# Columns of the modulation at another pace, summed two blocks past their request, and two later steps in the gates and the inverse

## The chip, the cores and the metric

The kernel runs on one core of a Trainium2 chip. The metric is the device time of one execution in microseconds (us). Before the change it is 1945.58 us, the median of three runs (1941.93 to 1946.73). A core has five engines with a queue of instructions each: TensorE (PE) for matmuls, VectorE (DVE), ScalarE (ACT), GpSimd (POOL) and SyncE (SP); here SP issues the transfers (DMA). Each engine works through its own queue in order, and waits at an instruction until what that instruction needs is there.

## The reference

One decoder layer for 256 positions of width 2048, in float32. Every part is normed and modulated by nine vectors of length 2048, which come from the conditioning `c` by one large matrix:

```python
x = x + 1/2 * gate1 * SwiGLU_1(mod(norm(x)))
x = x + gate2 * W_out [ FoX(heads 0..7) || GatedDeltaNet(heads 0..7) ]
x = x + 1/2 * gate3 * SwiGLU_2(mod(norm(x)))

# the gated delta rule, per head and chunk of 64
decay = jnp.exp(jnp.where(incl, g[..., :, None] - g[..., None, :], -jnp.inf))
lower = jnp.where(strict, jnp.einsum("bhnid,bhnjd->bhnij", kb, k) * decay, 0.0)
t_inv = lax.linalg.triangular_solve(eye + lower, jnp.broadcast_to(eye, lower.shape), ...)
u = t_inv @ vb
w = t_inv @ (kb * jnp.exp(g)[..., None])
```

A last norm follows. The decays `g` and the factors `beta` come from 24 extra columns of the mixer's input projection, through softplus and sigmoid: these are "the gates" below. The feed-forward parts are called FFN1 and FFN2, and what stands between them the mixer.

## The kernel before

**The weights** are cut into tiles of 128 x 128, and eight of them, in the order in which PE uses them, make a block of 512 KB. There are 674 blocks. For each, SP issues one transfer (`wraw`, line 125), ACT rounds it to the fast matmul format (`whi`, line 128), DVE forms the rest (`wlo = wraw - whi`, line 140), and PE multiplies with both halves. At most four buffers stand behind each of the three steps, with a few more for `wraw` in part of the kernel. So each block passes through four queues, and PE is late as soon as one `wlo` is.

Blocks 0 to 112 are the first gate/up part of FFN1 (28 pairs of feature tiles), 112 to 168 the down part for these, 168 to 232 the second gate/up part (16 pairs, four blocks each), 232 to 264 its down part. Blocks 264 to 378 are the mixer's input projection, 378 to 410 its output projection, 410 to 674 FFN2. In the profiled execution `wlo` of block 66 is made at 207 us, of 90 at 268, 112 at 330, 168 at 482, 232 at 659, 264 at 741, 378 at 1135 and 410 at 1229.

**The columns.** The matrix of the modulation is read as 142 columns of 1 MB (`adat`, line 262); each is multiplied by the conditioning and summed by one DVE instruction (line 266). `ada_col` requests a column; `Stream.next` calls it at a rate per block that the table `RATE` gives from block to block: 0.45 means 45 columns in 100 blocks. Where `W.late` is false, the sum is issued with the request; where it is true (from the mixer on), the sum is put into a list, and `settle` issues it behind `wlo` of the second block after (`BEHIND = 2`). The changed lines are in `Stream.next`, in the table, and in three lines of the mixer.

**The epilogue of a feature pair** in the second gate/up part: PE has left `pg` and `pu` (line 485 with `whi`, 486 with `wlo`), ACT copies one half to `mg` and DVE adds the other into `tg` and `tu` (497); ACT applies silu, DVE multiplies `tu` by `tg` (520), ACT rounds the product to `hid` and DVE forms its rest (504).

**The mixer.** While PE works through the projections, chains of small steps are dealt out between its tiles: Python generators for the gates and the keys ("k"), for each head of the delta rule ("gdn") and of the forgetting attention ("fox"), and for the output. Each `yield` names a gap in us by an internal clock that counts PE's tiles (`tick`, 0.35 us for each); a chain's next step is written down when that clock has passed its gap. A scheduling layer then orders the instructions of each engine by its own rules; `issue_after(i)` keeps an instruction behind instruction i in that order, `W.last` being the latest weight request and `W.split` the latest `wlo`.

- `gates` rounds the 24 extra columns (`x`, line 836), transposes them (`pcol`, 845), applies softplus and sigmoid, and sums with triangular matmuls (`prow`, 878).
- `decays`, `row_of` and `fetch_rows` (`rowd` to `rw`, 904, and to `x`, 929) make the decay matrices, with exponentials on ACT (918, 941).
- `keys` and `solve` make the lower triangle `Ln` for four heads at a time; `solve` sends its 16 x 16 blocks through memory (`ld`), inverts them by 15 products and reductions on DVE (1015, 1016), sends the result out (`lt<-x`, 1021) and back in another layout (`x<-lt`, 1025), and masks it into `U0` (1029). For the first half it then fetches the rows of the second (`x<-rowd`, 929).
- `gdn` of each head uses `U0`: `pu` (1051, 1053; another tile than the `pu` of FFN1), transposes `pvq` (1056) of the convolved queries and values `qv` (962, with silu on ACT), and goes on to `pn` (1093) and `put` (1105).
- `fox` of each head transposes its probabilities `ppt` (1209), which ACT made by an exponential (1204).

Of the kernel before, what the change touches and what calls it, by code (L numbers as in the profile page):

```python
# [13 lines left out]
ALU = mybir.AluOpType  # L14
# [18 lines left out]
GR = 24  # L33
NEG = -1e30

RATE = ((0, 0.5), (28, 0.25), (33, 0.5), (49, 0.25), (56, 0.5), (66, 0.2), (90, 0.0), (112, 0.5), (168, 0.45), (232, 0.26), (264, 0.0), (288, 0.295), (384, 0.0), (424, 0.16))
N_BIG, N_GDN = 3, 3
N_FIRST = 2
AHEAD = 4
# [4 lines left out]
LATER = 8  # L44
SLOTS = (3, 11)
BEHIND = 2

HA = 128 + 16
HS = 4 * HA
# [29 lines left out]
def woven(ap):  # L79

    return ap.rearrange("p (a b) -> p b a", a=2)
# [12 lines left out]
class Stream:  # L94


    def __init__(self, nc, w, raw, hi, lo):
        self.nc, self.w, self.raw, self.hi, self.lo = nc, w, raw, hi, lo
        self.order = []
        self.more = None  # L100
        self.h = self.l = self.last = None
        self.owed, self.side, self.quiet = 0.0, lambda: None, False
        self.tc, self.hold, self.held = None, None, []
        self.first = []
        self.lead = None
        self.late, self.owing = False, []

    def settle(self, upto=N_TILES):

# [21 lines left out]
    def next(self, mat, k, n, width=1):  # L131
        i = len(self.order)
        if i % WB == 0:
            nc = self.nc
            b = i // WB
            r, lo = self.first.pop(0) if self.first else self.block(b)
            self.l = lo.tile([P, WB * P], F32R, name="wlo")
            pace = [r_ for r_ in RATE if r_[0] <= b][-1][1]
            with self.behind():
                lo_ = nc.vector.tensor_tensor(self.l, r, self.h.bitcast(F32), ALU.subtract)  # L140
            with self.tc.issue_after(lo_.ins):
                self.settle(b - BEHIND)
            self.split = lo_.ins
            self.owed += 0.0 if self.quiet else pace
            while self.owed >= 1.0:
                self.owed -= 1.0
                self.side()
        for d in range(width):
            self.order.append((mat, k, n, width, d))
        o = (i % WB) * P  # L150
        h, l = self.h[:, o : o + width * P], self.l[:, o : o + width * P]
        return (h, l) if width == 1 else (woven(h), woven(l))
# [3 lines left out]
def layer_kernel(ctx: ExitStack, tc: tile.TileContext, xrow, c, adaw, cols, cst, w, out, order, dbg=None):  # L156
    nc = tc.nc
    V, A, G, PE = nc.vector, nc.scalar, nc.gpsimd, nc.tensor
# [18 lines left out]
    def psf(name="psf"):  # L177
        return sm2.tile([P, 512], F32, name=name, tag="psf")
# [6 lines left out]
    W = Stream(nc, w, raw, hi, lo)  # L185
# [40 lines left out]
    def C(name, lo_=0, n=None):  # L226
        o, wd = CST[name]
        return cstt[:, o + lo_ : o + (wd if n is None else lo_ + n)]

    def L(name, lo_=0, n=None):  # L230
        o, wd = COL[name]
        return colt[:, o + lo_ : o + (wd if n is None else lo_ + n)]
# [218 lines left out]
    def pt(name):  # L451
        return tmp.tile([P, T], F32, name=name, tag="pt", bufs=4)
# [301 lines left out]
    def mixer():  # L754
# [76 lines left out]
        def gates(ps):  # L831

            yr = x[:, 8]
            d = pt("ey")
            s = norm1.scaled(d, ps)
            A.activation(yr[R], d[R], AF.Identity, bias=s[R])
            y, ny, e, em, t0, q = (x[:, j, : 2 * GR].rearrange("p (t r) -> p t r", t=2) for j in range(10, KD))
            coef = tiny.tile([P, GR + PAD["hid"]], F32, name="coef", bufs=1)[:, :GR]
            tc.keep_in_program_order(A.activation(coef, L("alog"), AF.Exp))
            V.tensor_scalar(coef, coef, -1.0, None, ALU.mult)  # L840
            yield 4.0
            pc = psf("pcol")
            pcv = pc[:, : 2 * GR].rearrange("p (t r) -> p t r", t=2)
            for t in range(2):
                PE.transpose(pcv[:, t], yr[R, t * P : (t + 1) * P], ident[R, :GR])
            both = lambda c_: c_.unsqueeze(1).to_broadcast([P, 2, GR])
            V.tensor_tensor(y, pcv, both(L("gbias")), ALU.add)
            V.tensor_tensor(y, y, both(C("sgn")), ALU.mult)
            V.scalar_tensor_tensor(ny, y, -1.0, y, ALU.mult, ALU.min)
            A.activation(e, ny, AF.Exp)  # L850
            V.tensor_scalar(em, y, 0.0, None, ALU.min)
            A.activation(em, em, AF.Exp)

            S = ny
            V.tensor_scalar(t0, e, 2.0, None, ALU.add)
            V.reciprocal(t0, t0)
            V.tensor_tensor(S, e, t0, ALU.mult)
            V.tensor_tensor(t0, S, S, ALU.mult)
            V.tensor_scalar(q, t0, 1.0 / 17.0, None, ALU.mult)
            for n in (15, 13, 11, 9, 7, 5, 3):  # L860
                V.scalar_tensor_tensor(q, q, 1.0 / n, t0, ALU.add, ALU.mult)
            V.scalar_tensor_tensor(q, q, 1.0, S, ALU.add, ALU.mult)
            V.tensor_scalar(y, y, 0.0, None, ALU.max)
            V.scalar_tensor_tensor(y, q, 2.0, y, ALU.mult, ALU.add)
            V.tensor_tensor(y, y, both(coef), ALU.mult)

            V.tensor_scalar(t0, e, 1.0, None, ALU.add)
            V.reciprocal(t0, t0)
            V.tensor_tensor(colS[:, :, 4], em[:, :, 16:24], t0[:, :, 16:24], ALU.mult)
            yield 8.0  # L870

            fox_, gdn_ = slice(0, NH), slice(NH, 2 * NH)
            pr = psf("prow")
            po = psf("pcum")
            pcs = po[:, : 6 * NH].rearrange("p (t q r) -> p t q r", t=2, q=3)
            for t in range(2):
                sl = slice(t * P, (t + 1) * P)
                PE.matmul(pr[:NH, T + t * P : T + (t + 1) * P], y[:, t, gdn_], C("tri64"), start=True, stop=True)
                PE.matmul(pr[:NH, sl], y[:, t, fox_], C("tri"), start=True, stop=(t == 0))
                if t:  # L880
                    PE.matmul(pr[:NH, sl], y[:, 0, fox_], L("ones"), start=False, stop=True)
            for t in range(2):
                PE.matmul(pcs[:, t, 1], C("tri64"), y[:, t, gdn_], start=True, stop=True)
                PE.matmul(pcs[:, t, 2], C("tru64"), y[:, t, gdn_], start=True, stop=True)
                PE.matmul(pcs[:, t, 0], C("tri"), y[:, t, fox_], start=True, stop=(t == 0))
                if t:
                    PE.matmul(pcs[:, t, 0], L("ones"), y[:, 0, fox_], start=False, stop=True)
            rt = x[:, 8:10].rearrange("p a t -> p (a t)")[:NH]
            A.copy(rt, pr[:NH])
            nc.sync.dma_start(rows, rt)  # L890
            V.tensor_copy(colS[:, :, 0:2], pcs[:, :, 0:2])
            A.activation(colS[:, :, 2:4], pcs[:, :, 1:3], AF.Exp)
            V.tensor_tensor(nbeg, colS[:, :, 4], colS[:, :, 2], ALU.mult)
            V.tensor_scalar(nbt, colS[:, :, 4], -1.0, None, ALU.mult)
            V.tensor_scalar(ng, colS[:, :, 1], -1.0, None, ALU.mult)
            yield 2.0
            fetch_rows(0)
            yield 1.0
# [25 lines left out]
        def fetch_rows(half):  # L924

            rowk[half] = x[:, 4 * half : 4 * half + 4]
            src = rows[4 * half : 4 * half + 4, T:]
            with tc.issue_after(W.last):
                nc.sync.dma_start(rowk[half], src.unsqueeze(0).to_broadcast([P, 4, T]))
# [59 lines left out]
        def solve(half):  # L989


            hs4, n = slice(4 * half, 4 * half + 4), 2 * NH // 2
# [14 lines left out]
            blk, xt_, pr = (x[B, j] for j in range(4, 7))  # L1007
            with tc.issue_after(W.last):
                nc.sync.dma_start(blk, ld[ht].rearrange("n b e -> (n b) e"))
            yield 6.0  # L1010
            G.memset(xt_, 0.0)
            G.memset(xt_[:, 0:256:17], 1.0)
            bv, xv, pv = (t_.rearrange("p (i j) -> p i j", i=16) for t_ in (blk, xt_, pr))
            for i in range(1, 16):
                V.tensor_tensor(pv[:, :i, :i], xv[:, :i, :i], bv[:, i, :i].unsqueeze(1).to_broadcast([8 * n, i, i]), ALU.mult)
                V.tensor_reduce(xv[:, :i, i], pv[:, :i, :i], mybir.AxisListType.X, ALU.add)
                if i % 3 == 0:
                    yield 1.2
# [266 lines left out]
                if h + 1 < NH:  # L1285
                    rowf[h + 1] = row_of(h + 1, 0, "f")

        W.late = True
        first = project([("gt", 0)] + [("qkv", NH + h) for h in range(3)], norm1)
        start("k", -1, gates(first[0]))  # L1290
        for h in range(3):
            have_keys(h, first[1 + h], norm1)
# [37 lines left out]
    if dbg is None or "mix" in dbg:  # L1330
        mixer()
# [154 lines left out]
```

## Time and profile before

| what | value |
| --- | --- |
| median of three runs | 1945.58 us |
| the profiled execution | 1944.62 us, its span 1942.8 us |
| PE, share of the span | 98% |
| DVE | 81% |
| ACT | 54% |
| POOL | 3% |
| read from memory | 512.89 MB, 266 GB/s over the span |

The span is what the engines' records cover; the execution has 1.8 us around it. "Busy" counts records of work, not the time in which an engine waits at the head of its queue. A view of waits sums an engine's idle time by the instruction that stood and by what it stood for. A timeline has a row for each instruction with its start and its length, and in brackets the idle time ahead of it and what ended that.

### The profile page before, as it was taken

What the parts mean: (1) busy time and instruction counts of PE and PEld (TensorE: products, weight loads), DVE (VectorE), ACT (ScalarE), POOL (GpSimd) and SP (SyncE); (2) the same over time, 40 slices, a digit from 0 to 9 for tenths busy, and PEclk for the clock granted to TensorE, in tenths of its full rate; (3) what the DMA queues carried; (4) which work ended last, traced back from release to release, by engine and by line L of the source; (5) the groups of instructions that cost most, each with busy time, mean ns of one, the idle gap of its engine ahead of it and who ended that gap; (6) DMA issues with size and microseconds to landing.
All of it is one profiled execution on the core that took longest, in us unless ns stands there. A gap on an engine that the chain in (4) does not pass through costs nothing. (4 is left out here: it accounts for less than half of the span.)

```text
span 1942.8 us, 33800 instructions
## 1 busy us (share of the span) xinstructions
PE 1902.1 (98%) x13086; PEld 1774.6 (91%) x13087; DVE 1570.4 (81%) x2455; ACT 1047.1 (54%) x1668; POOL 53.5 (3%) x55
## 2 busy tenths in 40 slices
PE   9999999999999999999999999999999999999998
PEld 7999999988889899888989999999999999999997
DVE  6999978989999999878987989887777665666654
ACT  7444545433444557847656756665554445555553
POOL 0000000000000021000000002000000000000011
PEclk9999999999999999999999999999999999999999
DMA  9988867999999886585677557677777665666663
GB/s 376 354 348 329 325 227 257 399 377 375 365 360 366 327 287 225 199 333 198 207 275 274 204 196 247 203 256 275 263 262 251 227 204 198 203 199 202 200 201 120
DMA packets 129490, 519.58 MB, mean 267 GB/s; under 512 B 18217, under 2 KB 21545, under 8 KB 111153
## 3 DMA queue, kind: packets, MB, share of 16 engines
q1 hardware_dynamic: 129330, 517.42, 74.3%
q8 instruction: 103, 1.69, 0.3%
q14 instruction: 57, 0.47, 0.1%
HBM read 512.89 MB, written 4.47 MB: 266 GB/s over the span
## 5 line engine op out<-in xcount | busy, mean ns | idle before, releaser
L140 DVE TENSOR_TENSOR wlo<-wraw,whi 128x1024 fp32r<-128x1024 f32 x674 | 819.1, 1221 | 264.3 <-ACT whi L128 263.3
L128 ACT CAST whi<-wraw 128x1024 fp32r<-128x1024 f32 x674 | 698.9, 1044 | 523.3 <-PE pd L489 152.9
L489 PE MATMUL pd<-hid,whi 128*128 128x512 f32 x1408 | 461.7, 382 | 0.0
L490 PE MATMUL pd<-hid,wlo 128*128 128x256 f32 x1408 | 384.2, 273 | 2.1 <-DVE wlo L140 2.1
L266 DVE CUSTOM_DVE_ANT_0 adat<-adat,cs,colt 128x2048 f32<-128x2048 f32 x142 | 332.9, 2344 | 7.3 <-DMA adat<-in_ada_dram 7.3
L485 PE MATMUL pg<-hs,whi 128*128 128x512 f32 x912 | 302.7, 382 | 0.5 <-DVE shc L433 0.5
L485 PE MATMUL pu<-hs,whi 128*128 128x512 f32 x912 | 302.4, 382 | 0.0
L489 PEld LDWEIGHTS pd<-hid,whi 128*128 128x128 f32 x1408 | 266.3, 189 | 36.8
L490 PEld LDWEIGHTS pd<-hid,wlo 128*128 128x128 f32 x1408 | 270.3, 192 | 4.0 <-DVE wlo L140 3.9
L486 PE MATMUL pu<-hs,wlo 128*128 128x256 f32 x912 | 249.7, 274 | 5.8 <-DVE wlo L140 5.5
L486 PE MATMUL pg<-hs,wlo 128*128 128x256 f32 x912 | 249.8, 274 | 0.0
L571 PE MATMUL pgu<-hs,wlo 128*128 128x256 f32 x896 | 240.3, 278 | 7.5 <-DVE wlo L140 7.2
L569 PE MATMUL pgu<-hs,whi 128*128 128x256 f32 x896 | 245.0, 277 | 0.4 <-ACT whi L128 0.3
L570 PE MATMUL pgu<-hs,whi 128*128 128x256 f32 x896 | 244.5, 276 | 0.0
L485 PEld LDWEIGHTS pg<-hs,whi 128*128 128x128 f32 x912 | 172.6, 189 | 24.3 <-ACT shc L432 0.7
L485 PEld LDWEIGHTS pu<-hs,whi 128*128 128x128 f32 x912 | 172.6, 189 | 23.4
L486 PEld LDWEIGHTS pu<-hs,wlo 128*128 128x128 f32 x912 | 175.0, 192 | 8.6 <-DVE wlo L140 8.4
L571 PEld LDWEIGHTS pgu<-hs,wlo 128*128 128x128 f32 x896 | 168.6, 193 | 10.5 <-DVE wlo L140 10.4
L486 PEld LDWEIGHTS pg<-hs,wlo 128*128 128x128 f32 x912 | 175.1, 192 | 1.5
L569 PEld LDWEIGHTS pgu<-hs,whi 128*128 128x128 f32 x896 | 172.7, 193 | 1.1 <-ACT whi L128 0.5
L570 PEld LDWEIGHTS pgu<-hs,whi 128*128 128x128 f32 x896 | 172.8, 193 | 0.2 <-DVE hs L383 0.2
L798 PE MATMUL pp<-hs,whi 128*128 128x256 f32 x592 | 170.8, 289 | 0.2 <-ACT whi L128 0.2
(344 smaller groups left out, 2644.9 us busy)
## 6 DMA issues: line engine op xcount, KB each, us to landing
wraw<-in_w_dram SPq DMA_DIRECT2D x674, 512.0 KB, 4.4
adat<-in_ada_dram SPq DMA_DIRECT2D x142, 1024.0 KB, 7.9
xr<-in_xr_dram SPq DMA_DIRECT2D x4, 512.0 KB, 4.9
adaf<-in_ada_dram SPq DMA_DIRECT2D x4, 512.0 KB, 8.2
xd<-x SPq DMA_DIRECT2D x4, 512.0 KB, 7.2
rw<-rowd SPq DMA_DIRECT2D x16, 128.0 KB, 5.5
x<-xd SPq DMA_DIRECT2D x4, 512.0 KB, 5.3
out_dram<-o SPq DMA_DIRECT2D x8, 256.0 KB, 2.8
```

The costliest lines, as they stand in the source:

```text
L128: self.cast = self.nc.scalar.copy(self.h, r).ins
L140: lo_ = nc.vector.tensor_tensor(self.l, r, self.h.bitcast(F32), ALU.subtract)
L266: V.tensor_tensor_reduce(t, t, cs, 1.0, L("adab", q, 1), ALU.mult, ALU.add, mod[:, q : q + 1])
L485: PE.matmul(ps, wt[0], both, start=(k == 0), stop=False)
L486: PE.matmul(ps[:, T:], wt[1], part(k, HI), start=False, stop=(k == KD - 1))
L489: PE.matmul(ps, wt[0], act.rearrange("p q (a b) -> p q b a", a=2), start=first, stop=False)
L490: PE.matmul(ps[:, :T], wt[1], woven(act[:, 0]), start=False, stop=last)
L569: PE.matmul(o, wh, part(k, HI), start=first and s == 0, stop=False, skip_group_check=skip)
L570: PE.matmul(o, wh, part(k, LO), start=False, stop=False, skip_group_check=skip)
L571: PE.matmul(o, wl, part(k, HI), start=False, stop=last, skip_group_check=skip)
L798: PE.matmul(pp[i][:, :T], wh, hh, start=(k == 0), stop=False)
```

## The change

The table of rates has other values in three stretches: 0.2 columns per block go on from block 66 to 112 (before, to 90, and none from there to 112), 0.39 instead of 0.45 from 168 to 232, 0.25 instead of 0.26 from 232 to 264. In blocks 66 to 112 the sums come two blocks past the request, as they did from the mixer on. In the gates the internal clock's gap ahead of the transposes is 7 us for 4, in the inverse the gap ahead of its first product is 8 us for 6, and that product is kept behind the latest `wlo`.

```diff
-RATE = (... (56, 0.5), (66, 0.2), (90, 0.0), (112, 0.5), (168, 0.45), (232, 0.26), (264, 0.0), ...)
+RATE = (... (56, 0.5), (66, 0.2), (112, 0.5), (168, 0.39), (232, 0.25), (264, 0.0), ...)
+LATE = (66, 112)
-        self.late, self.owing = False, []
+        self.late, self.pinned, self.owing = False, False, []
@@ Stream.next
             b = i // WB
+            self.late = self.pinned or LATE[0] <= b < LATE[1]
@@ gates
-            yield 4.0
+            yield 7.0
             pc = psf("pcol")
@@ solve
-            yield 6.0
+            yield 8.0
             G.memset(xt_, 0.0)
             for i in range(1, 16):
-                V.tensor_tensor(pv[:, :i, :i], xv[:, :i, :i], bv[:, i, :i].unsqueeze(1).to_broadcast([8 * n, i, i]), ALU.mult)
+                with tc.issue_after(W.split) if i == 1 else nullcontext():
+                    V.tensor_tensor(pv[:, :i, :i], xv[:, :i, :i], bv[:, i, :i].unsqueeze(1).to_broadcast([8 * n, i, i]), ALU.mult)
@@ the mixer
-        W.late = True
+        W.late = W.pinned = True
```

Counted in DVE's order, the columns by stretches of blocks are, before and after: 29 and 29 up to block 66, 5 and 6 to 90, 1 and 4 to 112, 27 and 27 to 168, 29 and 25 to 232, 7 and 7 to 264, 28 and 29 to 410, 12 and 11 to 500, 4 and 4 to the end. ACT's order has 35 table loads before and 37 after. The changed kernel's line numbers are two higher, three from the inverse on.

DVE in the second gate/up part, before, from the 181st `wlo` on (the names carry buffer numbers; `adat` is a column's sum, which also reads out into `mod`):

```order
L140 TENSOR_TENSOR wlo_5959<-wraw_5955,whi_5957 128x1024
L497 TENSOR_TENSOR tu_5941<-pu_5845,mg_5945 128x256
L140 TENSOR_TENSOR wlo_5981<-wraw_5977,whi_5979 128x1024
L520 TENSOR_TENSOR tu_5941<-tu_5941,tg_5940 128x256
L504 TENSOR_TENSOR hid_5950<-tu_5941,hid_5950 128x256
L266 ISA adat_5983,mod_124<-adat_5983,cs_86,colt_87 128x2048
L266 ISA mod_124 128x1
L140 TENSOR_TENSOR wlo_6006<-wraw_6002,whi_6004 128x1024
```

The same place after the change, again from the 181st `wlo`:

```order
L142 TENSOR_TENSOR wlo_5968<-wraw_5964,whi_5966 128x1024
L268 ISA adat_5970,mod_124<-adat_5970,cs_86,colt_87 128x2048
L268 ISA mod_124 128x1
L499 TENSOR_TENSOR tu_5950<-pu_5857,mg_5954 128x256
L142 TENSOR_TENSOR wlo_5993<-wraw_5989,whi_5991 128x1024
L522 TENSOR_TENSOR tu_5950<-tu_5950,tg_5949 128x256
L142 TENSOR_TENSOR wlo_6015<-wraw_6011,whi_6013 128x1024
L506 TENSOR_TENSOR hid_5959<-tu_5950,hid_5959 128x256
L268 ISA adat_6017,mod_124<-adat_6017,cs_86,colt_87 128x2048
```

Before, one `wlo` stands between the evacuation of `tu` and the column; after, a column stands ahead of the evacuation, and the next one behind two `wlo`.

SP in the first half of the inverse, before, behind the 302nd weight request (`rw` and `rowd` are rows of the decays):

```order
L125 DMA wraw_9656<-in_w_dram 128x1024
L1021 DMA lt_8294<-x_85 64x256
L904 DMA rw_9689<-rowd_8288 128x256
L125 DMA wraw_9692<-in_w_dram 128x1024
L1025 DMA x_85<-lt_8294 128x8x16
L262 DMA adat_9698<-in_ada_dram 128x2048
L125 DMA wraw_9731<-in_w_dram 128x1024
L125 DMA wraw_9772<-in_w_dram 128x1024
L929 DMA x_85<-rowd_8288 128x4x256
L125 DMA wraw_9803<-in_w_dram 128x1024
```

The same steps after the change, behind the 307th request:

```order
L126 DMA wraw_9890<-in_w_dram 128x1024
L1024 DMA lt_8294<-x_85 64x256
L126 DMA wraw_9920<-in_w_dram 128x1024
L126 DMA wraw_9952<-in_w_dram 128x1024
L1028 DMA x_85<-lt_8294 128x8x16
L264 DMA adat_9958<-in_ada_dram 128x2048
L931 DMA x_85<-rowd_8288 128x4x256
L126 DMA wraw_10039<-in_w_dram 128x1024
```

The three steps stand five to six weight requests later. Two requests instead of one stand between `lt<-x` and `x<-lt`, and none instead of two between `x<-lt` and `x<-rowd`.

PE at the gates' transposes, before (`pp` is a projection, `pcol` the transposes):

```order
L798 MATMUL pp_8816<-hs_125,whi_8849 128x256
L799 MATMUL pp_8816<-hs_125,whi_8849 128x256
L845 MATMUL pcol_8776<-colt_87,x_85 128x24 x2
L800 MATMUL pp_8816<-hs_125,wlo_8851 128x256
L798 MATMUL pp_8816<-hs_125,whi_8849 128x256
```

And after the change:

```order
L800 MATMUL pp_8788<-hs_125,whi_8849 128x256
L801 MATMUL pp_8788<-hs_125,whi_8849 128x256
L847 MATMUL pcol_8819<-colt_87,x_85 128x24 x2
L802 MATMUL pp_8788<-hs_125,wlo_8851 128x256
L800 MATMUL pp_8788<-hs_125,whi_8849 128x256
```

Both stand behind the same number of PE instructions, and between the same two matmuls of the same tile.

More of the change, by code (lines that the diff above doesn't have):

```diff
@@ L34 @@
 NEG = -1e30
-RATE = ((0, 0.5), (28, 0.25), (33, 0.5), (49, 0.25), (56, 0.5), (66, 0.2), (90, 0.0), (112, 0.5), (168, 0.45), (232, 0.26), (264, 0.0), (288, 0.295), (384, 0.0), (424, 0.16))
+RATE = ((0, 0.5), (28, 0.25), (33, 0.5), (49, 0.25), (56, 0.5), (66, 0.2), (112, 0.5), (168, 0.39), (232, 0.25), (264, 0.0), (288, 0.295), (384, 0.0), (424, 0.16))
 N_BIG, N_GDN = 3, 3
```

## The prediction

> **What bounds the kernel now.** I read the busy shares first, then TensorE's waits, then a table by stretches of the span, and last the timelines of the three places where TensorE waits longest and the change acts.
>
> ```profile
> span 1942.8 us, 33800 instructions
> PE 1902.1 (98%) x13086; PEld 1774.6 (91%) x13087; DVE 1570.4 (81%) x2455; ACT 1047.1 (54%) x1668; POOL 53.5 (3%) x55
> ```
>
> TensorE (PE) is idle for 40.7 us of 1942.8 in all. The change takes no matmul away, so it can gain only from that idle time, or from time in which PE is busy at a lower clock. What PE waits for (us in total, times, longest us):
>
> ```profile
> PE pgu L571 <- DVE wlo L140: 7.2, 8, 2.7
> PE pu L486 <- DVE wlo L140: 5.5, 3, 2.0
> PE pvq L1056 <- ACT qv L962: 3.4, 3, 2.9
> PE ppt L1209 <- ACT x L1204: 2.3, 2, 2.2
> ...
> PE pcol L845 <- ACT x L836: 1.6, 1, 1.6
> ...
> PE prow L878 <- DVE x L865: 0.6, 1, 0.6
> ```
>
> The first row is work at the start of FFN1 and in FFN2, where the order does not change around the waits. The second is the second gate/up part of FFN1 (blocks 168 to 232, 482 to 660 us); the next two are one place of the mixer (835 to 886 us); the last two are the gates. By stretches:
>
> ```profile
> core 0: us, PE busy (x) PEld busy (x) DVE busy (x) ACT busy (x) POOL busy (x), PEclk, DMA share, GB/s
> 207.00:268.00 61.00, 61.00 (x549) 61.00 (x548) 53.51 (x81) 34.87 (x49) 0.00 (x0) 1.00 0.80 287
> 268.00:330.00 62.00, 62.00 (x558) 62.00 (x557) 48.49 (x80) 32.83 (x51) 0.00 (x0) 1.00 0.67 220
> 330.00:482.00 152.00, 149.90 (x920) 136.74 (x919) 143.51 (x169) 62.06 (x64) 0.00 (x0) 1.00 0.98 382
> 482.00:660.00 178.00, 172.25 (x1031) 155.11 (x1030) 164.21 (x190) 84.86 (x126) 0.00 (x0) 1.00 0.95 359
> 835.00:869.00 34.00, 31.74 (x230) 29.75 (x228) 28.28 (x43) 13.85 (x18) 0.00 (x0) 1.00 0.80 298
> 869.00:879.00 10.00, 7.28 (x59) 6.69 (x59) 6.76 (x22) 9.85 (x28) 0.42 (x2) 1.00 0.60 245
> 879.00:886.00 7.00, 5.52 (x27) 5.53 (x27) 4.61 (x4) 6.66 (x12) 0.00 (x0) 0.51 0.33 92
> ```
>
> Rows one and two are blocks 66 to 90 and 90 to 112: PE never idles there. Row three is the first down part. Row four loses 178.00 - 172.25 = 5.75 us. The last three lose 2.26 + 2.72 + 1.48 = 6.46 us of idle time, and 5.52 x (1 - 0.51) = 2.7 us more, since PE ran at half clock from 879: together 9.2 us.
>
> **Term 1, fewer columns in blocks 168 to 232.** The DVE timeline just ahead of a wait, and the wait:
>
> ```profile
> 516.77 0.42 DVE L497 TENSOR_TENSOR tu<-pu,mg 128x256 f32<-128x256 f32 x1 [0.98 <-ACT mg L496]
> 517.72 1.23 DVE L140 TENSOR_TENSOR wlo<-wraw,whi 128x1024 fp32r<-128x1024 f32 x1 [0.52 <-ACT whi L128]
> 518.86 0.42 DVE L520 TENSOR_TENSOR tu<-tu,tg 128x256 f32<-128x256 f32 x1
> 519.77 0.43 DVE L504 TENSOR_TENSOR hid<-tu,hid 128x256 fp32r<-128x256 f32 x1 [0.49 <-ACT hid L503]
> 520.11 2.35 DVE L266 CUSTOM_DVE_ANT_0 adat<-adat,cs,colt 128x2048 f32<-128x2048 f32 x1
> ...
> 522.38 1.22 DVE L140 TENSOR_TENSOR wlo<-wraw,whi 128x1024 fp32r<-128x1024 f32 x1
> 523.66 0.38 PE L486 MATMUL pu<-hs,wlo 128*128 128x256 f32 x1 [1.77 <-DVE wlo L140]
> ```
>
> The epilogue of one feature pair waits twice for ScalarE (0.52 and 0.49), then a column of 2.35 us goes ahead of the next wlo, and PE stands for 1.77 us. That pattern, a column behind hid with one wlo since tu, stands in the order three times in the stage, 20 blocks apart, and PE waits three times (5.5 us). In the changed order 25 columns stand in the stage instead of 29, and each has two wlo between the tu evacuation and itself, or none of the epilogue behind it. The three patterns are gone. So -5.5 us of waits, and 0.2 of the smaller idle time: **-5.7**. Bounds: -6.5 if the small waits behind also go; +2 if the column meets another epilogue by one late wlo of the same length; and 0 if the same three waits merely move.
>
> Cover: DVE has 164.21 of 178 busy and loses 4 x 2.345 = 9.4 us.
>
> ```profile
> L266 DVE CUSTOM_DVE_ANT_0 adat<-adat,cs,colt 128x2048 f32<-128x2048 f32 x29 | 68.0, 2345 | 0.0
> ```
>
> The next limit, the transfers, is not far: 359 GB/s at a share of 0.95, but the first down part moved 382 with PE busy for 149.90 of 152, and the stage now has 4 MB less to move.
>
> **Term 2, the columns go to blocks 66 to 112.** By the order one column more stands in blocks 66 to 90 and three more in 90 to 112. The latter then have the rate of the former: DVE 48.49 + 3 x 2.35 = 55.5 of 62, close to the 53.51 of 61 at which PE lost nothing. Summing two blocks past the request gives every transfer two blocks more to land.
>
> I take **0**; bounds 0 and +2.35 (one column that a wlo has to stand behind, undamped, at the turn into block 112). Between 330 and 482 us the columns are as many as before, one block shifted: 0.
>
> **Term 3, the gates' transposes.** The larger delay is written ahead of pcol, but in the order of PE the pcol row has not moved by one instruction, and what ScalarE and DVE do ahead of it neither:
>
> ```profile
> 780.44 0.30 PE L845 MATMUL pcol<-colt,x 24*128 24x24 f32 x2 [1.63 <-ACT x L836]
> ```
>
> So its 1.63 us stay: 0. What does move, by 1.4 blocks, is prow, whose wait of 0.6 us for DVE then has 3 us more: **-0.6**; bounds -0.6 and +0.6.
>
> **Term 4, the inverse later.** In the first half the chain begins on SP's queue, which runs in order:
>
> ```profile
> 847.06 0.38 DVE L1016 TENSOR_REDUCE x<-x 64x15 f32<-64x225 f32 x1
> 847.51 0.46 SPq L1021 DMA_DIRECT2D lt<-x  x1
> ...
> 849.46 0.38 SPq L1025 DMA_DIRECT2D x<-lt  x1
> 849.89 0.57 SPq L262 DMA_DIRECT2D adat<-in_ada_dram  x1
> 850.56 0.98 SPq L125 DMA_DIRECT2D wraw<-in_w_dram  x2
> 855.94 0.76 DVE L1029 TENSOR_TENSOR U<-x,cstt 128x256 f32<-128x256 f32 x2
> 856.72 0.38 SPq L929 DMA_DIRECT2D x<-rowd  x1
> 857.15 0.61 SPq L125 DMA_DIRECT2D wraw<-in_w_dram  x1
> ```
>
> lt<-x waits for the last reduction of the inverse, x<-rowd for U, and the weight requests queue behind both: 857.15 - 851.54 = 5.6 us without a request. ScalarE then stands for weights, and its later work bunches up into 867 to 883, with four table loads:
>
> ```profile
> ACT whi L128 <- DMA wraw<-in_w_dram: 17.3, 6, 5.1
> L962 ACT ACT_TABLE_LOAD x2 | 2.6, 1283 | 0.1
> L1204 ACT ACT_TABLE_LOAD x1 | 1.3, 1283 | 0.0
> L941 ACT ACT_TABLE_LOAD x1 | 1.3, 1283 | 0.0
> ```
>
> Hence ScalarE busy for 9.85 of 10 us, and PE's waits of 2.2 (ppt) and 2.9 (pvq). After the change the inverse's first product stands behind wlo 297 (was 293), lt<-x behind request 307 (was 302), x<-lt behind 309 (was 303), with x<-rowd right behind it. The casts that ran late now stand between the other ScalarE rows; pu and pvq go 1.3 to 1.6 blocks later on PE, while ppt, pn and put stay where they were. SP still stands from x<-lt to U, 856.72 - 849.46 = 7.3 us by these rows, now without the two requests that slipped through at 850.56. I take it that three waits remain: 0.3 ahead of the pfo transposes, 1.0 at pvq, and 2.5 at a wlo whose weight came late (between the rows 2.2 and 2.9); 3.8 us, and the half clock in one case of two, 1.4: 5.2 instead of 9.2, **-4.0**. Bounds: -9.2 if none remains, +3 if one wait of 2.9 is added to what there is.
>
> Beside the row of 0.51: the Trainium skill (TensorE: Matmul & The Clock Gate, What's actually happening) says that the gate halves the clock only after an idle window of about 3.4 us. Here it was half behind a wait of 2.9 us, so the trace speaks for less. By the page the 2.7 us would not hang on that wait and stay, the term would be 6.5 - 3.8 = -2.7, and the time 1.3 later.
>
> **Term 5, the rest of the mixer.** All of it is dealt out again from block 288 on, one column more falls into 264 to 410, and the order has 37 table loads for 35. Two loads are 2 x 1.283 = 2.6 us of an engine that is busy for 54%; where they fall into a bunch like the one above they count in full, elsewhere not at all. The second half's inverse also goes some three blocks later, with about 7.5 us of DVE work by the rows' lengths between its last reduction and U: enough for the 8.4 us from 847.51 to 855.94 but for 0.9. I take **+1.5**, bounds -1.5 (1.4, the wait for u at pk in this stretch, gone) and +5.
>
> ```profile
> PE pk L974 <- ACT u L1126: 1.4, 1, 1.4
> ```
>
> The Trainium skill (ScalarE: Activation LUTs, What ACT_TABLE_LOAD costs) puts a switch at 1.28 us of load and 1.38 us of drain, 2.66 in all; the rows have the 1283 ns, and 0.0 to 0.1 us of idle time ahead. By the page the two loads would be 5.3 us, and this term about 1.3 more.
>
> **Sum.** -5.7 + 0 - 0.6 - 4.0 + 1.5 = -8.8. The profiled execution took 1944.62 us (span 1942.8 and 1.8 around it); 1944.62 - 8.8 = 1935.8. The median of the runs shown, 1945.58, stood 0.96 above that execution: **1936.8, so 1937 us**.
>
> **The rivals.**
> - *The columns alone pay* (the mixer gives back as much as it gains: terms 4 and 5 together between -1 and +2): 1945.6 - 6.3 = 1939.3, so 1938.5 to 1942. For it: SP stands as long as before, and three consumers on PE have not moved. Against: the casts are spread.
> - *All of the mixer's waits go*: -5.7 - 0.6 - 9.2 + 0 = -15.5, 1930. For it: two requests more are out before SP stands. Against: ScalarE has as much work there, and a table load more.
> - *Slower: the chain from the inverse is late for PE.* Its start moved 4 blocks, its users on PE (pu, pvq) 1.3 to 1.6, pn and put not at all, so 2.5 to 4 blocks of slack are gone. If U comes after pu's turn, pu and put wait in each half, and the weights behind them. Priced by the row of 2.9 with its half clock, 2 x (2.9 + 2.7) = 11.2 a half: in the first 5.2 + 11.2 instead of 9.2 (+7.2), in the second +11.2. With one half -5.7 - 0.6 + 7.2 + 1.5 = +2.4, 1948; with both +13.6, 1959. It decides from the point where U lands later than pu is due. Against: U's two instructions end by 857.5 (855.94 and twice 0.76) and the first pu runs at 876, so 18 us of slack; 4 blocks at 172.25 / 64 = 2.7 us are 10.8.
>
> ```profile
> 876.00 0.38 PE L1051 MATMUL pu<-colt,U 128*64 128x128 f32 x2
> ```
>
> - *It does not do what it says*: the three waits of 168 to 232 reappear at other epilogues and the mixer stays even: 1944 to 1951. For it: the rate fell only from 0.45 to 0.39, and pcol did not move. Against: none of the three patterns is left in the order.
>
> **How the numbers follow.** Forecast (1934 to 1940) 0.44, columns alone 0.18, all waits gone 0.10, slower 0.17, no effect 0.11. About 0.3%, 5.8 us, is what a measurement of this kernel can tell: faster is below 1939.7, slower above 1951.4. Faster: 0.42 + 0.03 + 0.10 = 0.55. Same: 0.02 + 0.15 + 0.03 + 0.09 = 0.29. Slower: 0.14 + 0.02 = 0.16. The range goes from 1929.5 (all waits gone) to 1947 (no effect, its greater part), and leaves out the slower case and little else; the forecast's own range is 1934 to 1940.
>
> **What would show it.** Term 1: the row of pu waiting for wlo (5.5 us, 3 times) is gone, and blocks 168 to 232 take about 172 us. Term 2: PE busy throughout blocks 66 to 112. Term 3: pcol still waits some 1.6 us for x L836, prow no more. Term 4: the waits of ppt and pvq for ScalarE fall from 5.1 to under 2, with no half clock or one short one. Term 5: no PE wait over 2 us behind 886 us. The forecast is wrong if pu or put wait for U, if a new half-clock stretch shows in the mixer, or if wlo is late again in blocks 168 to 232.

## The result, and the profile after

| kernel | median | ratio to before, 95% interval |
| --- | --- | --- |
| before, 22 runs | 1944.61 us | |
| changed, 22 runs | 1941.27 us (1937.65 to 1947.69) | 0.9982 (0.9975 to 0.9989) |
| changed, again, 12 runs | 1943.54 us (1939.49 to 1949.54), beside 1944.74 | 0.9993 (0.9984 to 1.0002) |

The change is worth 1 to 3.5 us, less than the 0.3% that the prediction set as its bound for "faster", and the second interval reaches past 1. The first profile of the changed kernel fell on its longest execution (1947.69 us), so a second one, of the run "again", stands beside it. Its page begins with

```profile
span 1941.7 us, 33789 instructions
```

That is 1.1 us under the span before. The parts of the program show more than the sum. The table gives the time from the first matmul of one part to that of the next, read from the timelines of PE (the first column is the start of the first gate/up part):

| us | start | gate/up 1 | down 1 | gate/up 2 | down 2 | projection | output proj. | FFN2 |
| --- | --- | --- | --- | --- | --- | --- | --- | --- |
| before | 18.9 | 315.2 | 150.4 | 177.1 | 83.8 | 401.6 | 88.5 | 700.0 |
| after | 21.3 | 323.0 | 152.7 | 169.3 | 84.0 | 397.3 | 89.0 | 702.1 |
| again | 21.3 | 322.3 | 152.7 | 169.3 | 84.0 | 394.4 | 89.0 | 701.4 |

Gate/up 2 (blocks 168 to 232) saves 7.8 us, the projection 4.3 to 7.2. Gate/up 1 and down 1 together lose 9.4 to 10.1. The start differs by 2.4 us, but not because of the change (last section).

PE's waits in the changed kernel, first profile:

```profile
engine line waited for: us in total, times, longest us
PE pgu L573 <- DVE wlo L142: 13.9, 12, 2.7
PE pd L492 <- DVE wlo L142: 3.9, 8, 1.5
PE pvq L1059 <- ACT qv L964: 2.9, 1, 2.9
PE pd L491 <- DVE hid L506: 1.8, 1, 1.8
PE pcol L847 <- ACT x L838: 1.6, 1, 1.6
```

These are the five longest rows. The row of `pu` waiting for `wlo` (5.5 us) is gone, and so is `ppt`. In their place the first row has grown from 7.2 us to 13.9, and the second from 2.1 to 3.9. By stretches of the same profile:

```profile
core 0: us, PE busy (x) PEld busy (x) DVE busy (x) ACT busy (x) POOL busy (x), PEclk, DMA share, GB/s
207.00:272.00 65.00, 65.00 (x585) 65.00 (x584) 56.76 (x83) 33.91 (x49) 0.00 (x0) 1.00 0.77 285
272.00:346.00 74.00, 65.83 (x580) 64.77 (x578) 59.17 (x94) 36.02 (x56) 0.00 (x0) 1.00 0.73 256
...
497.00:666.00 169.00, 168.93 (x1025) 154.13 (x1024) 155.38 (x180) 83.65 (x125) 0.00 (x0) 1.00 0.93 351
...
872.00:892.00 20.00, 16.77 (x135) 16.39 (x134) 14.13 (x35) 15.86 (x37) 0.42 (x2) 0.91 0.80 284
```

The third row is gate/up 2 without a wait. The second is where blocks 90 to 112 were free of waits before: PE now idles there for 74.00 - 65.83 = 8.2 us. DVE isn't full (59.17 of 74). It is held up by columns that have not landed, as its own waits between 200 and 350 us say, after the change and before it:

```profile
DVE adat L268 <- DMA adat<-in_ada_dram: 15.5, 6, 3.6
```

```profile
DVE adat L266 <- DMA adat<-in_ada_dram: 1.3, 3, 0.7
```

One of the six, with the request of the column on SP and the PE wait behind it:

```profile
290.03 0.43 SPq L264 DMA_DIRECT2D adat<-in_ada_dram  x1
...
293.20 1.23 DVE L142 TENSOR_TENSOR wlo<-wraw,whi 128x1024 fp32r<-128x1024 f32 x1 [0.52 <-ACT whi L129]
298.03 2.35 DVE L268 CUSTOM_DVE_ANT_0 adat<-adat,cs,colt 128x2048 f32<-128x2048 f32 x1 [3.60 <-DMA adat<-in_ada_dram]
...
300.97 1.21 DVE L142 TENSOR_TENSOR wlo<-wraw,whi 128x1024 fp32r<-128x1024 f32 x1
302.24 0.38 PE L573 MATMUL pgu<-hs,wlo 128*128 128x256 f32 x1 [1.91 <-DVE wlo L142]
```

The request goes out at 290.03. The `wlo` ahead ends at 293.20 + 1.23 = 294.43, and from there on, 4.4 us after the request, DVE stands for that column. It gets it at 298.03, 8.0 us after the request, and the next `wlo` waits behind a column that isn't there yet: 3.60 us of waiting and 2.35 of summing in a row.

**Why the sums stand so early.** The text ahead of the prediction says of blocks 66 to 112 that the sums come two blocks past the request. That is what the edit writes, and not what the program does. In the first gate/up part `both` calls `ada_need(0, k)` for every tile, and `ada_need` ends with `W.settle()` without a bound, which empties the list of owed sums. So each sum is issued within one pair of tiles after its request is written, and not two blocks later. The scheduling layer then puts it where it thinks it ready: the column asked for behind the 101st weight request is summed behind the 98th `wlo`. The run with the rates alone (below) has no late sums ahead of the mixer, and up to block 264 its trace has the same rows on DVE, ACT and SP as that of the changed kernel, in the same order. **The part of the change that names itself "late" has no effect there**; what acts is the table of rates, and the mixer's edits.

### The profile page after: what moved, and what is told of

The parts are those of the page before. It is cut to its first block, busy times and chain, and to the rows that moved or that the text cites. A ratio compares the mean times of both kernels' runs of the same rounds, so it can differ in the third digit from the quotient of the medians.

```text
span 1945.9 us, 33788 instructions
## 1 busy us (share of the span) xinstructions
PE 1903.2 (98%) x13086; PEld 1773.5 (91%) x13087; DVE 1568.8 (81%) x2455; ACT 1049.9 (54%) x1670; POOL 54.5 (3%) x55
## 4 chain that ended last, share of the span: by engine, by line
PE 72%; DVE 13%; DMA 6%; issue 5%; ACT 3%; SPq 0%; DVEq 0%; ACTq 0%
PE pd L491 14%; PE pg L487 10%; PE pu L487 10%; PE pd L492 7%; PE pg L488 5%; PE pu L488 5%; DVE wlo L142 5%; DVE adat L268 3%; PE po L491 3%; DMA adat<-in_ada_dram 3%; DMA wraw<-in_w_dram 2%; PE pgu L573 2%; PE pgu L572 2%; PE pgu L571 2%; PE po L492 1%
## 5 line engine op out<-in xcount | busy, mean ns | idle before, releaser
L573 PE MATMUL pgu<-hs,wlo 128*128 128x256 f32 x896 | 240.7, 279 | 14.3 <-DVE wlo L142 13.9
```

The lines of the kernel that those rows point to most:

```text
L573: PE.matmul(o, wl, part(k, HI), start=False, stop=last, skip_group_check=skip)
```

## The experiments

**The changed kernel again**, for a second profile. No edit.

> The changed kernel once more, with a second profile. Theory W (the columns that moved to blocks 90 to 112 are summed too early: DVE stands for their transfers, and PE for the wlo behind): PE waits for wlo between blocks 90 and 114 come to 7 to 9 us again, DVE stands for adat some 15 us in blocks 66 to 114, and the time is 3 to 4 us under before. Rival V (the profile shown was an unlucky execution, 1947.69 us where the median is 1941.27): the same waits come to less than 3 us in this profile.

DVE's wait for `adat` between 200 and 355 us was 14.8 us in 6 times, PE's waits there were 6.1 (pgu) and 1.5 (pd): theory W, on a run that was 4 us shorter than the first. The loss is no accident of one execution. The time was 1.2 us under before, less than the 3 to 4 expected.

**The rates alone.**

```diff
 before
-(66, 0.2), (90, 0.0), (112, 0.5), (168, 0.45), (232, 0.26)
+(66, 0.2), (112, 0.5), (168, 0.39), (232, 0.25)
```

> Before, with the new table of rates alone (sums as before, gates and inverse as before). Theory W: blocks 168 to 232 save 7 to 8 us and blocks 90 to 114 lose 8 to 9.5, so the time is within 2 us of before (ratio 0.999 to 1.001), and the gain of the change comes from the mixer's edits. Rival M (the columns pay, the mixer's edits give nothing): 3 to 6 us under before (0.997 to 0.9985).

1944.77 us beside 1944.74, ratio 1.0001 (0.9992 to 1.0009). The parts: gate/up 1 324.8, down 1 152.7, gate/up 2 169.3, projection 396.4. So 7.8 us saved in gate/up 2 cost 11.9 in gate/up 1 and down 1; 1.7 of these are a half clock of 3.41 us at 321 us, which the changed kernel does not have there. The rates pay nothing, as theory W has it. New is that the projection fell by 5.2 us, though no line of the mixer was edited: one column more falls into it, and from block 300 to 378 the rows of DVE stand in another order than before.

**The mixer's edits alone.**

```diff
 before
-            yield 4.0        # gates
+            yield 7.0
-            yield 6.0        # solve
+            yield 8.0
+                with tc.issue_after(W.split) if i == 1 else nullcontext():
```

> Before, with the three edits of the gates and the inverse alone, rates as before. Theory W: 3 to 5 us under before (ratio 0.9975 to 0.9985), the three waits of pu for wlo in blocks 168 to 232 still there (5 to 6 us). Rival M: within 1.5 us of before.

1939.24 us, ratio 0.9974 (0.9963 to 0.9984): 5 to 5.5 us, just past the upper edge of theory W. Gate/up 2 took 177.1 as before, with its three waits of `pu`, the projection 394.8 instead of 401.6. It is faster than the whole change, which took 1943.54 in the same set of runs.

**Sums that stand two blocks later in fact.** `ada_need` settles only when the column it needs is still owed:

```diff
 the changed kernel
-            W.owing.append((len(W.order) // WB, total))
+            W.owing.append((len(W.order) // WB, total, i))
-        W.settle()
+        if W.pinned or (W.owing and W.owing[0][2] <= ada_seq.index((m, j))):
+            W.settle()
```

> The changed kernel, in which a need for a column that is summed already no longer empties the list of owed sums before the mixer, so that the sums of blocks 66 to 112 do stand two blocks past the request. Theory W: DVE's wait for adat there falls from 15 us to under 2, PE's waits for wlo in blocks 90 to 114 from about 8 us to under 2, and the time is 6 to 9 us under the changed kernel, 9 to 13 under before (ratio 0.9935 to 0.9955). Rival V: the time is that of the changed kernel within 2 us.

1935.25 us, ratio 0.995 (0.9938 to 0.9962). In the order the column asked for behind request 101 is now summed behind `wlo` 103. Between 207 and 355 us DVE doesn't wait for `adat` at all, and of PE's waits one is left:

```profile
engine line waited for: us in total, times, longest us
PE pd L493 <- DVE wlo L142: 1.8, 1, 1.8
```

Gate/up 1 is back at 315.1 with the same columns but for one, which falls behind block 112 now. So it was the place of the sums, five `wlo` earlier than here, that cost 7 to 8 us there, and not their work.

**Late sums up to block 118, and up to block 264.** The wait that is left comes from the column asked for at block 113, the first that is again summed at once.

```diff
 late_true
-LATE = (66, 112)
+LATE = (66, 118)        # late_118
+LATE = (66, 264)        # late_264
```

> late_true, with the late sums up to block 118 and not 112, so that the column asked for at block 113 is not summed ahead of its wlo. Theory W: PE's wait of 1.8 us for wlo at block 114 goes, and the time is 1 to 2.5 us under late_true (ratio 0.993 to 0.9945). Rival: the wait moves to the first column that is again summed at once, near block 120, and the time stays within 1 us of late_true.

> late_true, with the late sums up to block 264, through the down part (112 to 168) and the second gate/up part. Theory W: as late_118, and the small waits for wlo in blocks 112 to 168 (3.8 us beyond the matmuls' own time) fall to about 2: 2 to 4 us under late_true (ratio 0.9925 to 0.994). Rival: a column two blocks late falls behind hid again in blocks 168 to 232, the waits of 1.8 to 2 us come back there, and the time is that of late_true or up to 4 us above it.

late_118 took 1931.22 us, ratio 0.9931 (0.9917 to 0.9945): 4 us under late_true, more than expected. In the two profiles down 1 fell from 153.1 to 150.4 (the wait of 1.8 at block 114 gone), and the rest is the start (last section) and the projection, 396.7 to 394.3: there late_true has two half clocks of 3.41 us, with DVE's rows from block 300 to 378 in the same order, so that this part need not be the edit's. late_264 took 1932.03, ratio 0.9934 (0.9922 to 0.9947), with down 1 at 149.4 and gate/up 2 at 169.4: no difference from late_118 that can be told. Behind block 118 the place of the sums made none. late_118 is faster than both kernels. The first line of its page, and PE's waits:

```profile
span 1929.4 us, 33795 instructions
```

```profile
PE pgu L574 <- DVE wlo L142: 7.2, 8, 2.7
PE pvq L1060 <- ACT qv L965: 2.8, 1, 2.8
PE pd L493 <- DVE wlo L142: 2.1, 6, 0.6
PE pcol L848 <- ACT x L839: 1.6, 1, 1.6
```

The rows of `wlo` are those of before, 7.2 and 2.1, without `pu`'s 5.5.

**The gates alone, and the inverse alone.** Each half of the mixer's edit on the kernel before.

> Before, with the gates' gap of 7 alone. The three mixer edits together gave 5.1 us (ratio 0.9974). Theory I (the inverse's place carries it, since SP stands less long ahead of weights): within 1.5 us of before, pcol's wait of 1.6 us as before, prow's 0.6 gone. Rival G (the gates' part, softplus and prow 1.4 blocks later, carries it): 3 to 5 us under before.

> Before, with the two edits of the inverse alone (gap of 8, first product behind the latest wlo). Theory I: 3 to 5 us under before (ratio 0.9975 to 0.9985), with ppt's wait of 2.2 us gone and the half clock at 879 us shorter or gone. Rival G: within 1.5 us of before.

gates_only took 1936.94 us, 0.9964 (0.9951 to 0.9976), inverse_only 1938.14, 0.997 (0.9958 to 0.9981), beside 1944.56. Neither theory held: each alone gives as much as both or more, so the gains don't add. PE's waits from 835 to 892 us, in before (two more rows of 0.2 left out), gates_only, inverse_only and rates_only, each in a fence of its own:

```profile
PE pvq L1056 <- ACT qv L962: 2.9, 1, 2.9
PE ppt L1209 <- ACT x L1204: 2.3, 2, 2.2
PE pp L800 <- DVE wlo L140: 0.8, 1, 0.8
...
```

```profile
PE pvq L1056 <- ACT qv L962: 1.6, 1, 1.6
PE ppt L1209 <- ACT x L1204: 0.3, 2, 0.2
```

```profile
PE pp L800 <- DVE wlo L140: 1.4, 3, 0.6
PE pfo L1216 <- ACT x L1212: 1.1, 1, 1.1
PE ppt L1210 <- ACT x L1205: 0.4, 2, 0.2
```

```profile
PE pfo L1215 <- ACT x L1211: 3.6, 1, 3.6
PE pvq L1056 <- ACT qv L962: 1.7, 1, 1.7
```

By these rows before has 6.0 us of waits, and 6.83 us of half clock from 879.08 on; gates_only has 1.9, inverse_only 2.9, rates_only 5.3, and none of the three a half clock in that place. ACT's wait for weights there was 17.3 us before, and 10.2, 8.9 and 11.0 in the three. Three edits that have nothing in common but that they shift the steps against each other each take 5 to 8 us off the projection (401.6 to 393.7, 394.3 and 396.4). What was special was how the steps met in the kernel before, not the edit.

**The old rates, with the sums of blocks 168 to 232 moved.** This tells apart why gate/up 2 got faster.

```diff
 before, with late_true's ada_need and the change's line in Stream.next
+LATE = (168, 232)
```

> Before, with its own rates and the mixer as before, and with sums that do stand two blocks past the request in blocks 168 to 232 alone. The stage keeps 28 of its 29 columns, but none of them stands right behind hid with one wlo since tu. Theory P (the prediction's: that place makes the three waits of pu for wlo): the waits of 5.5 us go, and the time is 5 to 7 us under before (ratio 0.9965 to 0.9975). Theory N (two columns two wlo apart around one epilogue are too much work for DVE, wherever they stand; the lower rate is what helps): three waits of 1 to 2 us stay in the stage, 3 to 6 us in all, and the time is within 2 us of before, but for what a re-ordered mixer brings.

1946.09 us beside 1945.48, ratio 1.0007 (0.9998 to 1.0016). PE's waits in the stage:

```profile
PE pu L489 <- DVE wlo L142: 3.6, 3, 1.2
```

As theory N has it, three waits stay, 1.2 us each instead of 1.8 to 2.0, and gate/up 2 takes 175.7 us against 177.1, with 28 columns instead of 29. Also, down 2 lost 2.3 us. In the projection the rows of DVE and SP stand as before, one for one from block 300 to 378, and it took 402.6 us, with `ppt` and `pvq` at 3.0 and 2.9 and half clock again: what the kernel before shows there belongs to its order, and comes back with it.

**late_118 with the transposes moved in fact**, and **with the inverse's edits taken back.**

```diff
 late_118
-            yield 7.0
+            yield 13.0        # pcol_13
-                PE.transpose(pcv[:, t], ...)
+                with tc.issue_after(W.mm):        # the latest matmul of the projection
+                    PE.transpose(pcv[:, t], ...)
```

> late_118 with the gates' transposes moved in fact: a gap of 13 and the transposes kept behind the latest matmul of the projection, so that on PE they stand 11 tiles later. Theory: pcol's wait of 1.6 us for x L838 goes, and the time is 1 to 2 us under late_118 (ratio 0.992 to 0.993) if the mixer's later places stay as they are. Rival: prow, the decays and the inverse come later with it and the mixer waits elsewhere: from late_118's time to 4 us above it.

> late_118 with the two edits of the inverse taken back, the gates' gap of 7 kept. If the inverse's edits carry part of the gain, 2 to 4 us above late_118 (ratio 0.994 to 0.9955); if any re-ordering of that place does as well (the gates alone gave 7.0 us, the inverse alone 5.8, both 5.1), within 2 us of late_118 (0.992 to 0.994).

pcol_13 took 1935.02 us, 0.9949 (0.9936 to 0.9961), 3.8 above late_118: the rival. The wait at `pcol` is gone, and the one wait of the gates is now

```profile
790.47 0.38 PE L882 MATMUL prow<-cstt,x 128*8 128x128 f32 x2 [2.54 <-DVE x L869]
```

```profile
791.00:799.00 8.00, 8.00 (x43) 7.71 (x42) 3.44 (x8) 3.75 (x5) 0.00 (x0) 0.57 0.65 192
```

The second is the window behind it (PE, PEld, DVE, ACT and POOL busy, the granted clock, the share and rate of the DMA): PE busy throughout, at a granted clock of 0.57. The wait only moved along the gates' chain, and grew. late_gates took 1932.6, 0.993 (0.9918 to 0.9943): within 1.4 us of late_118, as expected if any order but that of before will do.

## Why the prediction was right in its range, and where it was wrong

The measured time lay in the range, and the direction was right. The likeliest case was not what happened: 8.6 us were forecast against the median of the runs shown, and 1 to 3.5 came. By its own bounds (faster is below 1939.7) the result is "same", to which it gave 0.29, and not "faster" with 0.55. That the time lies in the range is luck in part: with the loss of about 10 us in a term put at 0, the sum of -8.8 would have come to +1, and larger gains than forecast in gate/up 2 and the projection made up for it.

- **Term 1, fewer columns in blocks 168 to 232: -5.7 forecast, -7.8 measured.** The three waits went, and the smaller idle time with them. It passed the bound of -6.5: the sum counted only the matmuls' idle time, and the weight loads ahead of them (PEld, `pu` from `wlo`) stood 8.4 us for `wlo` in the profile before and 1.2 after. The mechanism was half right. The prediction named the place of a column, behind `hid` with one `wlo` since `tu`. place_168 takes away that place, keeps 28 of the 29 columns, and keeps three waits of 1.2 us. The changed order also still has that pattern three times (the prediction said none), and PE waits at none of them. So the lower rate removes the waits (rates_only, with 169.3 us, has none either), and the place alone does not make them. Theory N's own reason, two columns two `wlo` apart around one epilogue, is not shown either: the changed order has such a pair (the rows from the 181st `wlo` on, ahead of the prediction) without a wait. Why just three epilogues of before were late stays open.
- **Term 2, the columns in blocks 66 to 112: 0 forecast, with bounds 0 and +2.35; +9.4 to +10.1 measured.** This is the step that failed. It counted DVE's work, which does fit, put the wait for the transfer at nothing, and took the edit's word for that: "Summing two blocks past the request gives every transfer two blocks more to land". The order that was at hand showed the sum behind `wlo` 98 and its request behind weight 101, and the comparison at the same rate in blocks 66 to 90 was misleading: there the sums stand up to two `wlo` ahead of their request, here three. DVE then stood 15.5 us for six columns. late_true shows that nothing else was wrong: with the sums two behind, the term is 0 in gate/up 1, and with block 113 too (late_118), 0 in down 1.
- **Term 3, the gates.** pcol didn't move and kept its 1.6 us, as read from the order. prow's 0.6 went, but a `wlo` two blocks later waited 0.7 in its place (798 us): 0 and not -0.6.
- **Terms 4 and 5, the inverse and the mixer: -2.5 forecast together, -3.1 with prow; -4.3 and -7.2 measured in the projection in two profiles**, and +1.4 to +2.1 in FFN2, where PE waited 1.8 us for `hid` behind a column that waited 2.21 us for its transfer (1.1 and 1.5 in "again"). The waits of ppt and pvq fell from 5.1 to 2.9 and 1.6, with a short half clock once. In one profile the size was near; the cause was not: the rates alone or the gates alone do the same without the inverse's later place. The account of SP's queue may describe how the kernel before got into that state, but it doesn't say which edit gets it out. The price was also misread at one point: the half clock from 879.08 began inside the wait for `pvq` (880.48 - 2.92 = 877.56 to 880.48), not behind it.
- **The rival that the columns alone would pay** is refuted the other way round, though 1941.27 lies among its times: the columns gave 1.0001, the mixer's edits 0.9974.
- **The slower case** (the chain from the inverse late for PE) didn't show: no wait of PE for `solve`'s `U` is among its waits. Of the prediction's signs of being wrong two did, in small: `put` waited 1.0 us in all for the `U` that its own chain makes (line 1098; 0.2 before), and "again" has a new half clock at the gates (below).

The Trainium skill (TensorE: Matmul & The Clock Gate, What's actually happening) was weighed with its window of about 3.4 us. The traces bear out its length (steps of 3.413 us, below), but neither that PE has to stand for a whole window nor the price of the slower case, a half clock for every wait of 2.9. Half clock came behind waits of 2.54 (above) and, in "again", 1.63 us; and it did not come behind 3.58 us in rates_only:

```profile
784.64 0.30 PE L847 MATMUL pcol<-colt,x 24*128 24x24 f32 x2 [1.63 <-ACT x L838]
```

```profile
878.95 0.49 PE L1215 MATMUL pfo<-x 128*128 128x128 f32 x2 [3.58 <-ACT x L1211]
```

The traces' records of the granted clock say more. In all thirteen profiles the clock changes only at steps of 3.413 us: up to its last change, each stretch at one clock lasts a whole number of them (1, 2, 27, 197, 225, ...). Here are the windows of the steps that hold each wait, and of the steps behind it, in "again", pcol_13 and rates_only (columns as above):

```profile
782.00:785.41 3.41, 1.78 (x16) 1.55 (x15) 3.41 (x6) 3.08 (x6) 0.00 (x0) 1.00 0.65 228
785.41:788.82 3.41, 3.41 (x18) 3.41 (x17) 2.66 (x11) 3.31 (x7) 0.00 (x0) 0.50 0.78 265
```

```profile
788.41:791.83 3.42, 1.36 (x12) 0.99 (x12) 3.42 (x11) 1.99 (x4) 0.00 (x0) 1.00 0.63 196
791.83:798.65 6.82, 6.82 (x33) 6.82 (x34) 2.62 (x7) 3.63 (x5) 0.00 (x0) 0.50 0.61 175
```

```profile
873.71:877.13 3.42, 1.66 (x15) 1.47 (x14) 1.04 (x1) 2.11 (x3) 0.00 (x0) 1.00 1.04 432
877.13:880.54 3.41, 1.59 (x14) 1.59 (x15) 3.41 (x6) 3.35 (x9) 0.42 (x2) 1.00 1.00 405
880.54:883.95 3.41, 3.41 (x33) 3.41 (x32) 3.41 (x4) 3.28 (x9) 0.00 (x0) 1.00 0.63 211
```

The wait of 3.58 falls on two steps, with 1.76 and 1.82 us of idle time, and costs no clock. Of the wait of 2.54, 2.06 fall into one step, and the clock halves. Over the thirteen profiles all 30 steps at full clock in which PE stood for 1.99 us or more were followed by half clock, none with less than 1.62 was, and of the 26 between 8 were. (The ends of matmuls are modelled, so these limits are rough; the 1.63 us at `pcol` are among the 26, and went either way.) So here about 2 us of standing within one step are enough, and it matters how a wait falls on the steps, not its length alone. The same section calls the window free-running, which fits: the steps lie elsewhere against the program in each profile (last section).

## What to carry to other kernels

An edit that moves work "later" has moved it only if the order of the built program says so: look at where a consumer stands against its own request, in rows of the same queue, before costing the edit, and look at every call that may flush a list early. A consumer whose turn comes 4 us after its request, where the transfer takes 5 to 8 (5.4 to 8.3 in the changed kernel between 200 and 350 us), holds up all that is behind it, though the engine has room on average. And where several unrelated edits of a tangled stretch all give the same gain, the stretch before was probably unlucky; take such a gain as one draw, and don't add it up.

## What was not expected of the hardware

The start of the program takes 18.8 to 19.1 us or 21.0 to 21.3 until the first product of gate/up 1, and nothing between, over thirteen profiles: four of the first kind (before, yields_only, late_118, late_264) and nine of the second, with old and new rates in both. The row that differs is the same eight matmuls, in before and in after:

```profile
5.47 4.05 PE L670 MATMUL pcs<-crow,one 1*128 1x512 f32 x8
```

```profile
5.61 7.19 PE L672 MATMUL pcs<-crow,one 1*128 1x512 f32 x8
```

The nine slow starts begin these matmuls at 5.60 or 5.61 us, the four fast ones at 4.84 to 5.47, in programs that haven't begun to differ. It makes 2.4 us, most of what the change was worth, so single profiles of this kernel can't be compared by their spans.

The records of the clock go with it. In the four, the first record of full clock begins at 3.99 to 5.27 us, just ahead of these matmuls; in the nine only at 16.69 to 17.43, behind them. Counted back from there in steps of 3.413 us, a step begins at 3.04 to 3.78 us in the nine. So the kind of start goes with where the steps of the clock lie against the program's start, which no edit sets; no run moved the start on purpose.
